# One modulation vector: sums on VectorE and a few selecting products in place of many narrow TensorE products

## The chip, the cores and the metric

The kernel runs on one core of one Trainium2 chip. The metric is the device time of one execution in microseconds (us). Three executions of the kernel before took 1913.95, 1915.27 and 1922.95 us; the median is 1915.27 us.

## The reference, cut to what matters

A two-layer backbone works on 256 latent tokens and 256 context tokens of width 2048. Each layer starts with a modulation:

```
mod   = silu(c)     @ mod_w[layer] + mod_b[layer]     # mod_w[layer]: 2048 x 6144
mod_c = silu(c_ctx) @ mod_w[layer] + mod_b[layer]
shift, scale, gate       = split(mod, 3)
shift_c, scale_c, gate_c = split(mod_c, 3)
h_lat = rms_norm(x)   * (1 + scale)   + shift
h_ctx = rms_norm(ctx) * (1 + scale_c) + shift_c
```

Layer 0 is a Hyena long convolution beside an S5 scan, layer 1 a differential attention. All is float32. The change touches one product only: the `scale` part of layer 1 (a 2048 x 2048 block of `mod_w[1]`), for the two streams latent (`c`) and context (`c_ctx`). It needs layer 1's weights and the two conditioning vectors and nothing else, so it can be worked out at any time before layer 1 begins.

## The kernel before, in words

Large products go by `project` and `rows`: a weight tile of 512 KB (128 partitions x 1024) is fetched on the SyncE queue into `raw` (three buffers), ScalarE rounds it to `whi` (L174), VectorE subtracts to `wlo` (L175), and TensorE makes three products (`mm3`, L108 to L110) of 512 columns for each of the tile's 8 pieces of 128 rows. `whi` and `wlo` have three buffers each, so VectorE can be at most some two to three tiles ahead of TensorE. A `unit` of layer 0's input projection is two such tiles, and in a `hp` unit two VectorE instructions of the short convolution after them (L760, L761).

Beside the units runs the generator `late()` (L708). It makes 48 steps: for layer 0's gate, layer 1's shift and layer 1's scale (`(layer, r)` = (0, 2), (1, 0), (1, 1)), for four blocks j of 512 columns, four steps i of 512 rows. A step first uses the two tiles `gw` of 512 KB that the step before had fetched, then asks for the next two; `gw` has two buffers, so a tile can be fetched only when the instructions that read its predecessor are done. Before the change a step is 16 calls of TensorE in `quarters` (L580): 128 rows of weights against the 32 columns of `cst` (columns 0 and 1 are the two streams), each for one quarter of 128 columns, into one PSUM bank `aux`. After four steps ScalarE copies the bank to the row `mrow` (L733). After four blocks `modulation` transposes it (L595) and adds the bias (L598, L624). Steps are started by `fill` inside `project`: half a step at each of a unit's two tiles while the Hyena stage runs, so about one step a unit.

The stage in which the last 16 steps (layer 1's scale) run is 718 to 965 us of the span: the end of the second of four Hyena quarters, ten units alone, then the last two Hyena quarters with the last units, then the start of the S5 gate (`glu`, whose tiles are multiplied by the pairs `gh`, `gl`).

The program is a fixed order of instructions for each engine, chosen when it is built. Each engine works through its own order and waits at the head of it; the same holds for the SyncE queue that issues the transfers. The gates of layer 1 are summed in the attention (L1142, L1144) by the same VectorE instruction that the change now uses for the scale.

Of the kernel before, what the change touches and what calls it, by code (L numbers as in the profile page):

```python
# [15 lines left out]
MULT, ADD, SUB = ALU.mult, ALU.add, ALU.subtract  # L16
# [128 lines left out]
def rsqrt(k, x, shape, tag):  # L145
    v = k.nc.vector
    y, t = k.t(shape, tag + "y", bufs=2), k.t(shape, tag + "t", bufs=2)
    k.nc.scalar.activation(t, x, AF.Sqrt)
    v.reciprocal(y, t)
    v.tensor_tensor(t, y, y, op=MULT)  # L150
    v.tensor_tensor(t, t, x, op=MULT)
    v.tensor_scalar(t, t, -0.5, 1.5, op0=MULT, op1=ADD)
    v.tensor_tensor(y, y, t, op=MULT)
    return y
# [341 lines left out]
def hybrid_kernel(ctx: ExitStack, tc: tile.TileContext, A, out):  # L496
    nc = tc.nc
    v, act, pe, dma = nc.vector, nc.scalar, nc.tensor, nc.sync
# [3 lines left out]
    k = K(tc, main, psum)  # L502

    def phase(name):
        class Phase:
            def __enter__(s):
                s.p = tc.tile_pool(name=name, bufs=1)
                k.pools.append(s.p.__enter__())

            def __exit__(s, *a):  # L510
                k.pools.pop()
                return s.p.__exit__(*a)
        return Phase()
# [15 lines left out]
    act.dma_start(pick, A["pick"])  # L529
    ones = k.m([128, 128], "ones")  # L530
    v.memset(ones, 1.0)
    even = phase("even")
    even.__enter__()
    P = k.e([128, 2, 8, 2, 4, 9], "s5P")
# [32 lines left out]
    def conditioning():  # L567

        t = k.e([128, 16, 32], "cst")
        v.memset(t, 0.0)  # L570
        for s in range(2):
            act.activation(t[:, :, s], cc[:, 16 * s:16 * s + 16], AF.Silu)
        return t

    cst = conditioning()

    def quarters(b, kk, w, first=0, last=15):

        for q in range(4):
            pe.matmul(b[32 * q:32 * q + 32, :128], cst[:, kk], w[:, q * 128:q * 128 + 128], start=kk == first, stop=kk == last)  # L580

    def modulation(layer, r, m):

        if r == 2:
            gate_rows(layer, m)
            return
        mods[layer, r] = (mod_scale if r else mod_columns)(layer, r, m)
# [88 lines left out]
    def project(W, col, h, lo_tok=0, n_tok=512, steps=0):  # L676

        b = k.bank("acc")
        nk = len(h)
        for kk, hi, lo in cols128(W, col, nk):  # L680
            s = slice(lo_tok, lo_tok + n_tok)
            mm3(nc, b[:, :n_tok], (hi, lo), (h[kk][0][:, s], h[kk][1][:, s]), kk == 0, kk == nk - 1)
            if kk % (nk // 2) == 0:
                fill(steps)
        return b
# [21 lines left out]

    def late():  # L708

        steps = [(layer, r, j, i) for layer, r in ((0, 2), (1, 0), (1, 1)) for j in range(4) for i in range(4)]  # L710

        def load(layer, r, j, i):
            ws = []
            for z in (2 * i, 2 * i + 1):
                w = k.e([128, 2, 512], "gw", bufs=GW)
                c0 = r * 2048 + j * 512
                dma.dma_start(w, A["mod_w"][layer][z * 256:z * 256 + 256, c0:c0 + 512].rearrange("(a p) m -> p a m", p=128))
                ws += [(2 * z + a, w[:, a]) for a in range(2)]
            return ws

        ws = load(*steps[0])
        for n, (layer, r, j, i) in enumerate(steps):
            yield
            if i == 0:
                b = k.bank("aux")
                if j == 0:
                    m = k.e([128, 512], "mrow", bufs=1)
            for kk, w in reversed(ws):
                quarters(b, kk, w, 3, 12)
            if n + 1 < len(steps):  # L730
                ws = load(*steps[n + 1])
            if i == 3:
                act.copy(m[:, j * 128:j * 128 + 128], b[:, :128])  # L733
                if j == 3:
                    modulation(layer, r, m)
        yield

    rest = late()

    due = [0]  # L740
# [34 lines left out]
    with phase("start"):  # L775
# [13 lines left out]
        for i, w in enumerate((w1, w2)):  # L789
            b = k.bank("wk")  # L790
            pe.matmul(b[:64, :256], w, prev, start=True, stop=True)
            z = k.t([64, 256], "hyz")
# [10 lines left out]
        for w in BLOCKS:  # L803
            c0 = sum(BLOCKS[:len(blocks)])
            blocks.append((c0, w))
            for r in (1, 0):
                kk = 0
# [178 lines left out]
    with phase("hyena"):  # L986
# [4 lines left out]
        for q in range(4):  # L991
# [20 lines left out]
            for i in range(2):  # L1012
# [3 lines left out]
                for part in range(2):  # L1016
                    bs = []
                    for e in range(2):
                        b = k.bank("wk")
# [38 lines left out]
            for c in range(2):  # L1058
                b = k.bank("tp", [128, 2, 2, 128])
# [17 lines left out]
    with phase("glu"):  # L1077
# [14 lines left out]
        for ct in range(8):  # L1092
            sg = k.t([128, 512], "sg", bufs=2)
            dma.dma_start(sg, spill["sg", ct])
            b = project(A["s5_glu_w"][0], ct * 128, gp)
# [27 lines left out]
    for i in range(2):  # L1123
        w = nw[:, i]
        v.tensor_tensor(tab[:, i, 0], rope[:, 0], w[:, None, :].to_broadcast([128, 2, 64]), op=MULT)
        for z in range(2):
            ws = w.rearrange("p (h z j) -> p h z j", h=2, z=2)[:, :, 1 - z][:, None].to_broadcast([128, 2, 2, 16])
# [116 lines left out]
    with phase("attention"):  # L1244
        hl = [x[1] for x in h]
        om = []
        for c in range(4):
# [6 lines left out]
            for hd in range(4):  # L1254
                b = project(W_in, 6144 + (c * 4 + hd) * 128, hl, 0, 256)
# [3 lines left out]
                for qt in range(2):  # L1259
                    z = k.t([128, 2], "z", bufs=4)  # L1260
                    mx = k.t([128, 2], "mx", bufs=4)
                    ps = []
                    for m in range(2):
                        b = k.bank("wk")
# [15 lines left out]
                for qt in range(2):  # L1280
                    qs = slice(qt * 128, qt * 128 + 128)
                    b = k.bank("wk")
# [3 lines left out]
                    r = k.t([128, 1], "or", bufs=2)  # L1286
                    act.activation(o2, b[:, :128], AF.Square, accum_out=r)
                    v.tensor_scalar(r, r, 1.0 / 128.0, EPS, op0=MULT, op1=ADD)
                    r = rsqrt(k, r, [128, 1], "ors")
# [33 lines left out]
def build(nc, inputs):  # L1323
    arrays, aps = {}, {}
    for name, a in list(inputs.items()) + list(constants().items()):
        a = np.ascontiguousarray(a)
        arrays[f"in_{name}_dram"] = a
        aps[name] = nc.dram_tensor(f"in_{name}_dram", a.shape, mybir.dt.from_np(a.dtype), kind="ExternalInput").ap()
    out = nc.dram_tensor("out_0_dram", (1, N, D), F32, kind="ExternalOutput").ap()
    with tile.TileContext(nc) as tc:  # L1330
        hybrid_kernel(tc, aps, out)
    return arrays
# [10 lines left out]
```

## Time and profile before

| what | value |
|---|---|
| median of three runs | 1915.27 us |
| the profiled execution | 1924.88 us |
| its span, first to last instruction | 1922.7 us |
| TensorE busy | 1841.3 us (96%) |
| VectorE busy | 1333.8 us (69%) |
| ScalarE busy | 790.2 us (41%) |
| mean granted TensorE clock | 0.988 of full speed |
| narrow products of L580 from `gw` | 2048 instructions, 88.9 us busy |

Matmuls overlap in their records, so what one costs is read from the distance between starts, not from its duration. A float32 product is two instructions in the trace: a step of 16 calls shows as 32. VectorE instructions overlap a little too.

### The profile page before, as it was taken

The page shows a single profiled execution, that of the slowest core. Times are in us where ns is not written, and L with a number is a line of the kernel's source. Part 1 is how long each engine was busy: PE and PEld are TensorE (multiplying, and loading weights), DVE is VectorE, ACT ScalarE, POOL GpSimd, SP SyncE. Part 2 cuts the span into 40 slices and gives each one's busy share as a digit, 9 for nine tenths or more (in the row PEclk, how much of TensorE's full clock was granted, in tenths as well). Part 3 has the DMA queues.
Part 4 walks back from the last instruction along what each step waited for, and adds up shares of the span by engine and source line. Part 5 has one row for each costly group of instructions (what it writes and reads, how often), then busy time and mean ns, then how long its engine had stood idle before and what let it go on. Part 6 is the DMA issues. An engine that isn't in the chain of part 4 may idle for free.

```text
span 1922.7 us, 30952 instructions
## 1 busy us (share of the span) xinstructions
PE 1841.3 (96%) x12101; PEld 1454.8 (76%) x12101; DVE 1333.8 (69%) x2563; ACT 790.2 (41%) x1245; POOL 7.0 (0%) x23
## 2 busy tenths in 40 slices
PE   4799899999999999999999999999999999999998
PEld 3577677777676677777788887779778878887977
DVE  4887768998985586258664347686866867768675
ACT  3342223222223332233352237537735833853762
POOL 0000000000000000000000000000000000000000
PEclk8899899999999999999999999999999999999999
DMA  9878655676875776564657345354336426435356
GB/s 302 263 248 265 215 147 164 181 236 200 246 226 149 247 236 194 187 210 157 215 188 234 113 139 178 100 167 139 103 107 186 121 88 190 131 96 170 127 178 227
DMA packets 325572, 349.57 MB, mean 182 GB/s; under 512 B 53417, under 2 KB 204459, under 8 KB 325427
## 3 DMA queue, kind: packets, MB, share of 16 engines
q1 hardware_dynamic: 314144, 339.84, 56.1%
q10 hardware_dynamic: 10850, 5.93, 1.2%
q8 instruction: 95, 1.56, 0.3%
q0 software_dynamic: 432, 1.84, 0.3%
q14 instruction: 51, 0.41, 0.1%
HBM read 316.06 MB, written 31.48 MB: 181 GB/s over the span
## 4 chain that ended last, share of the span: by engine, by line
PE 67%; DMA 4%; DVE 2%; ACT 1%; issue 1%; SPq 0%; ACTq 0%; DVEq 0%
PE ps_acc L108 14%; PE ps_acc L109 13%; PE ps_acc L110 13%; PE ps_aux L108 5%; PE ps_aux L109 5%; PE ps_aux L110 5%; DMA gw<-in_mod_w_dram 2%; PE ps_aux L580 2%; PE ps_wk L1266 2%; PE ps_wk L1284 2%; PE ps_wk L108 1%; PE ps_tp L1277 1%; PE ps_wk L109 1%; DVE wlo L175 1%; PE ps_wk L110 1%
## 5 line engine op out<-in xcount | busy, mean ns | idle before, releaser
L174 ACT CAST whi<-raw 128x1024 fp32r<-128x1024 f32 x304 | 318.8, 1049 | 640.6 <-PE ps_acc L109 341.1
L175 DVE TENSOR_TENSOR wlo<-raw,whi 128x1024 fp32r<-128x1024 f32 x304 | 371.4, 1223 | 303.0 <-ACT whi L174 298.7
L108 PE MATMUL ps_acc<-hhi,whi 128*128 128x512 f32 x768 | 313.9, 410 | 0.1
L109 PE MATMUL ps_acc<-hlo,whi 128*128 128x512 f32 x768 | 308.7, 402 | 0.2
L110 PE MATMUL ps_acc<-hhi,wlo 128*128 128x512 f32 x768 | 307.7, 401 | 0.0
L108 PEld LDWEIGHTS ps_acc<-hhi,whi 128*128 128x128 f32 x768 | 145.3, 190 | 42.7 <-issue 10.5
L110 PEld LDWEIGHTS ps_acc<-hhi,wlo 128*128 128x128 f32 x768 | 145.2, 189 | 34.6 <-issue 2.0
L109 PEld LDWEIGHTS ps_acc<-hlo,whi 128*128 128x128 f32 x768 | 145.3, 189 | 34.1 <-issue 3.2
L108 PE MATMUL ps_acc<-whi,hhi 128*128 128x512 f32 x416 | 165.9, 399 | 1.2 <-DVE qt L1167 0.9
L109 PE MATMUL ps_acc<-wlo,hhi 128*128 128x512 f32 x416 | 163.9, 394 | 0.0
L580 PE MATMUL ps_aux<-gw,cst 128*32 128x128 f32 x2048 | 88.9, 287 | 34.5 <-DMA gw<-in_mod_w_dram 30.3
L580 PEld LDWEIGHTS ps_aux<-gw,cst 128*32 128x32 f32 x2048 | 56.7, 113 | 69.2 <-DMA gw<-in_mod_w_dram 38.3
L108 PE MATMUL ps_aux<-whi,h 128*128 128x512 f32 x256 | 100.0, 393 | 4.8 <-DVE qt L1167 4.8
L109 PE MATMUL ps_aux<-wlo,h 128*128 128x512 f32 x256 | 101.1, 395 | 0.0
L110 PE MATMUL ps_acc<-whi,hhi 128*128 128x512 f32 x256 | 100.4, 392 | 0.0
L110 PE MATMUL ps_aux<-whi,h 128*128 128x512 f32 x256 | 100.4, 392 | 0.0
L108 PEld LDWEIGHTS ps_acc<-whi,hhi 128*128 128x128 f32 x416 | 78.2, 188 | 21.1 <-DVE qt L1167 2.9
L109 PEld LDWEIGHTS ps_acc<-wlo,hhi 128*128 128x128 f32 x416 | 78.3, 188 | 15.0
L110 PE MATMUL ps_acc<-whi,hlo 128*128 128x512 f32 x224 | 88.2, 394 | 0.0
L109 PE MATMUL ps_acc<-h,whi 128*128 128x256 f32 x256 | 72.7, 284 | 0.0
L108 PE MATMUL ps_acc<-h,whi 128*128 128x256 f32 x256 | 72.7, 284 | 0.0
L110 PE MATMUL ps_acc<-h,wlo 128*128 128x256 f32 x256 | 72.7, 284 | 0.0
(414 smaller groups left out, 3495.9 us busy)
## 6 DMA issues: line engine op xcount, KB each, us to landing
gw<-in_mod_w_dram SPq DMA_DIRECT2D x128, 512.0 KB
raw<-in_od_in_w_dram SPq DMA_DIRECT2D x128, 512.0 KB
raw<-in_ev_in_w_dram SPq DMA_DIRECT2D x96, 512.0 KB
raw<-in_ev_out_w_dram SPq DMA_DIRECT2D x40, 512.0 KB
hhi<-in_mod_w_dram SPq DMA_DIRECT2D x64, 256.0 KB
qt<-in_mod_w_dram SPq DMA_DIRECT2D x64, 256.0 KB
raw<-in_od_out_w_dram SPq DMA_DIRECT2D x32, 512.0 KB
spill_hp<-out SPq DMA_DIRECT2D x24, 256.0 KB
```

Of the source, the lines that this page charges most:

```text
L108: nc.tensor.matmul(out, lh, rh, start=start, stop=False)
L109: nc.tensor.matmul(out, lh, rl, start=False, stop=False)
L110: nc.tensor.matmul(out, ll, rh, start=False, stop=stop)
L174: k.nc.scalar.copy(hi, src)
L175: k.nc.vector.tensor_tensor(lo, src, hi.bitcast(F32), op=SUB)
L580: pe.matmul(b[32 * q:32 * q + 32, :128], cst[:, kk], w[:, q * 128:q * 128 + 128], start=kk == first, stop=kk == last)
L1266: pe.matmul(b, qT[m][part][:, hd, qt * 128:qt * 128 + 128], kT[m][:, hd], start=part == 0, stop=part == 1)
L1277: pe.transpose(tb[:, t], ps[0][:, t * 128:t * 128 + 128], ident)
L1284: pe.matmul(b[:, :128], wT[qt][:, t], vt[:, t, hd * 128:hd * 128 + 128], start=t == 0, stop=t == 3)
```

## The change

For `(layer, r)` = (1, 1) a step no longer calls `quarters`. VectorE keeps, for each of the 128 rows of a tile and each of the two streams, a running sum over the 16 pieces of 128 weight rows: `acc[row, stream, column]`, a tile of 128 x 2 x 512 that takes the place of `P` (tag `s5P`, one buffer). That is 8 instructions a step (4 pieces, 2 streams) on 512 columns: 2 of `tensor_scalar` at the start of each block j, else `scalar_tensor_tensor`. At the end of a block 8 products with `sel` (128 x 32, all zero but a column of ones at the stream's place) add up the 128 rows by quarters into the bank, which is now taken only there. The rest (copy, transposes, bias) is as before.

```diff
+    sel = k.m([128, 2, 32], "sel")
+    v.memset(sel, 0.0)
+    for s in range(2):
+        v.memset(sel[:, s, s:s + 1], 1.0)
...
             if i == 0:
-                b = k.bank("aux")
+                if (layer, r) != (1, 1):
+                    b = k.bank("aux")
+                else:
+                    acc = k.e([128, 2, 512], "s5P")
                 if j == 0:
                     m = k.e([128, 512], "mrow", bufs=1)
-            for kk, w in reversed(ws):
-                quarters(b, kk, w, 3, 12)
+            for z, (kk, w) in enumerate(reversed(ws)):
+                if (layer, r) != (1, 1):
+                    quarters(b, kk, w, 3, 12)
+                    continue
+                for s in range(2):
+                    if i == z == 0:
+                        v.tensor_scalar(acc[:, s], w, cst[:, kk, s:s + 1], None, op0=MULT)
+                    else:
+                        v.scalar_tensor_tensor(acc[:, s], w, cst[:, kk, s:s + 1], acc[:, s], op0=MULT, op1=ADD)
             if n + 1 < len(steps):
                 ws = load(*steps[n + 1])
+            if i == 3 and (layer, r) == (1, 1):
+                b = k.bank("aux")
+                for s in range(2):
+                    for q in range(4):
+                        pe.matmul(b[32 * q:32 * q + 32, :128], sel[:, s], acc[:, s, q * 128:q * 128 + 128], start=s == 0, stop=s == 1)
             if i == 3:
                 act.copy(m[:, j * 128:j * 128 + 128], b[:, :128])
```

How the order moves is shown at two places. (Line numbers of the changed kernel are 20 higher behind the change: L780 is L760, L1091 is L1071, L599 is L595; L744 and L742 are the new sums, L751 the selecting product.)

The first place is the fourth step of block 0, among the units that run alone (765 to 838 us in the trace before). VectorE there, before: two tiles and a convolution, over and over.

```order
L175 TENSOR_TENSOR wlo_7957<-raw_7954,whi_7956 128x1024
L760 SCALAR_TENSOR_TENSOR out_7861<-ps_acc_7780,pk_558_2737,out_7861 128x2x255
L761 SCALAR_TENSOR_TENSOR out_7861<-ps_acc_7780,pk_558_2737,out_7861 128x2x255
L175 TENSOR_TENSOR wlo_8008<-raw_8005,whi_8007 128x1024
L175 TENSOR_TENSOR wlo_8044<-raw_8041,whi_8043 128x1024
```

VectorE there, now (`gw_7710` and `gw_7708` are the third step's two tiles, `gw_7788` and `gw_7786` the fourth's; `s5P_7620` is the running sum of block 0):

```order
L175 TENSOR_TENSOR wlo_7938<-raw_7935,whi_7937 128x1024
L780 SCALAR_TENSOR_TENSOR out_7841<-ps_acc_7768,pk_559_2741,out_7841 128x2x255
L744 SCALAR_TENSOR_TENSOR s5P_7620<-gw_7708,cst_111,s5P_7620 128x512
L781 SCALAR_TENSOR_TENSOR out_7841<-ps_acc_7768,pk_559_2741,out_7841 128x2x255
L744 SCALAR_TENSOR_TENSOR s5P_7620<-gw_7708,cst_111,s5P_7620 128x512 x3
L175 TENSOR_TENSOR wlo_7981<-raw_7978,whi_7980 128x1024
L744 SCALAR_TENSOR_TENSOR s5P_7620<-gw_7788,cst_111,s5P_7620 128x512 x4
L175 TENSOR_TENSOR wlo_8017<-raw_8014,whi_8016 128x1024
L780 SCALAR_TENSOR_TENSOR out_7929<-ps_acc_7846,pk_559_2741,out_7929 128x2x255
L744 SCALAR_TENSOR_TENSOR s5P_7620<-gw_7786,cst_111,s5P_7620 128x512
L781 SCALAR_TENSOR_TENSOR out_7929<-ps_acc_7846,pk_559_2741,out_7929 128x2x255
L744 SCALAR_TENSOR_TENSOR s5P_7620<-gw_7786,cst_111,s5P_7620 128x512 x3
```

Every `wlo` but the first of these now stands behind four sums, and the sums behind a transfer of `gw`. TensorE at the same place, before, with a step's 16 calls between two products of a tile:

```order
L110 MATMUL ps_acc_7953<-hhi_794,wlo_7957 128x512
L580 MATMUL ps_aux_7963<-gw_7894,cst_107 32x128 x8
L580 MATMUL ps_aux_7963<-gw_7892,cst_107 32x128 x8
L108 MATMUL ps_acc_7953<-hhi_806,whi_7956 128x512
L109 MATMUL ps_acc_7953<-hlo_807,whi_7956 128x512
```

TensorE there, now:

```order
L110 MATMUL ps_acc_7934<-hhi_1836,wlo_7981 128x512
L751 MATMUL ps_aux_7868<-s5P_7620,sel_85 32x128 x4
L108 MATMUL ps_acc_7934<-hhi_1848,whi_7980 128x512
L109 MATMUL ps_acc_7934<-hlo_1849,whi_7980 128x512
L751 MATMUL ps_aux_7868<-s5P_7620,sel_85 32x128 x4
L110 MATMUL ps_acc_7934<-hhi_1848,wlo_7981 128x512
```

The steps' calls are gone, and block 0's selecting products stand behind the first products of the tile `wlo_7981`, while the last sums they read stand on VectorE behind the tile after it, `wlo_8017`.

The second place is the end of the last Hyena quarter and the beginning of the S5 gate (about 937 to 960 us in the trace before). VectorE before (`part`, `hyt`: the last Hyena instructions; `gl`: the low halves of the gate's inputs):

```order
L1071 TENSOR_TENSOR hyt_8874<-part_8680,hyt_8874 128x512
L175 TENSOR_TENSOR wlo_9431<-raw_9428,whi_9430 128x1024
L175 TENSOR_TENSOR gl_9223<-g_9220,gh_9222 128x512
L175 TENSOR_TENSOR wlo_9472<-raw_9469,whi_9471 128x1024
L175 TENSOR_TENSOR gl_9229<-g_9226,gh_9228 128x512
L175 TENSOR_TENSOR gl_9235<-g_9232,gh_9234 128x512
```

VectorE there, now:

```order
L1091 TENSOR_TENSOR hyt_8816<-part_8622,hyt_8816 128x512
L744 SCALAR_TENSOR_TENSOR s5P_8469<-gw_8840,cst_111,s5P_8469 128x512 x4
L744 SCALAR_TENSOR_TENSOR s5P_8469<-gw_8838,cst_111,s5P_8469 128x512 x4
L175 TENSOR_TENSOR gl_9142<-g_9139,gh_9141 128x512
L175 TENSOR_TENSOR gl_9148<-g_9145,gh_9147 128x512
L175 TENSOR_TENSOR gl_9154<-g_9151,gh_9153 128x512
L742 TENSOR_SCALAR s5P_8992<-gw_8916,cst_111 128x512 x2
L744 SCALAR_TENSOR_TENSOR s5P_8992<-gw_8916,cst_111,s5P_8992 128x512 x2
L744 SCALAR_TENSOR_TENSOR s5P_8992<-gw_8914,cst_111,s5P_8992 128x512 x4
L175 TENSOR_TENSOR gl_9160<-g_9157,gh_9159 128x512
L175 TENSOR_TENSOR gl_9166<-g_9163,gh_9165 128x512
```

The last step of block 2 and the first of block 3 have come to stand between the Hyena stage and the gate's inputs. TensorE there, before, at the gate's first tile:

```order
L595 MATMUL ps_tp_9369<-ident_79,mrow_7617 128x128 x3
L108 MATMUL ps_acc_9427<-gh_9222,whi_9430 128x512
L109 MATMUL ps_acc_9427<-gl_9223,whi_9430 128x512
L110 MATMUL ps_acc_9427<-gh_9222,wlo_9431 128x512
L108 MATMUL ps_acc_9427<-gh_9228,whi_9430 128x512
```

TensorE there, now:

```order
L1082 MATMUL ps_tp_8806<-ident_79,hyt_8797 128x128
L599 MATMUL ps_tp_9281<-ident_79,mrow_7621 128x128 x2
L751 MATMUL ps_aux_8918<-s5P_8469,sel_85 32x128 x8
L108 MATMUL ps_acc_9339<-gh_9141,whi_9342 128x512
L599 MATMUL ps_tp_9281<-ident_79,mrow_7621 128x128
L109 MATMUL ps_acc_9339<-gl_9142,whi_9342 128x512
```

Block 2's selecting products stand right behind the last Hyena transposes and ahead of every product of the gate.

## Rows read from the trace of the kernel before

**Rows 1.** The page: busy time by engine, and busy tenths in 40 slices.
```profile
PE 1841.3 (96%) x12101; PEld 1454.8 (76%) x12101; DVE 1333.8 (69%) x2563; ACT 790.2 (41%) x1245; POOL 7.0 (0%) x23
...
PE   4799899999999999999999999999999999999998
...
DVE  4887768998985586258664347686866867768675
```
**Rows 2.** Stretches: PE, PEld, DVE, ACT, POOL busy (instructions), clock, DMA share, GB/s.
```profile
765.00:838.00 73.00, 73.00 (x453) 57.80 (x450) 19.58 (x20) 15.54 (x19) 0.00 (x0) 1.00 0.62 195
838.00:965.00 127.00, 125.43 (x764) 96.49 (x764) 93.47 (x109) 46.65 (x66) 0.00 (x0) 1.00 0.61 197
...
718.00:965.00 247.00, 245.43 (x1496) 190.37 (x1496) 144.63 (x166) 77.05 (x102) 0.00 (x0) 1.00 0.61 196
```
**Rows 3.** Waits in 718 to 965 us: us in total, times, longest.
```profile
DVE wlo L175 <- ACT whi L174: 69.5, 24, 5.6
...
PE ps_aux L580 <- DMA gw<-in_mod_w_dram: 1.6, 1, 1.6
```
**Rows 4.** TensorE in order of time around one step: start, us, instruction.
```profile
763.62 0.40 PE L110 MATMUL ps_acc<-hhi,wlo 128*128 128x512 f32 x1
763.94 1.08 PE L580 MATMUL ps_aux<-gw,cst 128*32 128x128 f32 x32
764.95 0.50 PE L108 MATMUL ps_acc<-hhi,whi 128*128 128x512 f32 x1
765.29 0.39 PE L109 MATMUL ps_acc<-hlo,whi 128*128 128x512 f32 x1
765.52 0.40 PE L110 MATMUL ps_acc<-hhi,wlo 128*128 128x512 f32 x1
```
**Rows 5.** In order of time: one tile's split among the lone units.
```profile
769.92 1.05 ACT L174 CAST whi<-raw 128x1024 fp32r<-128x1024 f32 x1 [5.04 <-PE ps_acc L109]
771.00 1.23 DVE L175 TENSOR_TENSOR wlo<-raw,whi 128x1024 fp32r<-128x1024 f32 x1 [4.09 <-ACT whi L174]
```
**Rows 6.** TensorE's group of narrow products in 718 to 965 us.
```profile
L580 PE MATMUL ps_aux<-gw,cst 128*32 128x128 f32 x512 | 19.5, 277 | 1.6 <-DMA gw<-in_mod_w_dram 1.6
```
**Rows 7.** Sums of layer 1's gate: ns min/median/max; in time; their waits.
```profile
L1142 DVE TENSOR_SCALAR gsum<-qt,sc x4: 485/486/488, 1278.7 to 1757.0; 128x512 f32<-128x512 f32 x4
...
1292.84 3.11 DVE L1144 SCALAR_TENSOR_TENSOR gsum<-qt,sc,gsum 128x512 f32<-128x512 f32 x4
...
DVE gsum L1144 <- DMA qt<-in_mod_w_dram: 16.8, 12, 2.0
```
**Rows 8.** VectorE in order of time: independent instructions one behind the other.
```profile
750.63 0.68 DVE L1065 TENSOR_TENSOR part<-ps_tp,part 128x512 f32<-128x512 f32 x1
751.22 0.74 DVE L761 SCALAR_TENSOR_TENSOR out<-ps_acc,pk,out 128x510 f32<-128x510 f32 x1
751.88 0.68 DVE L1065 TENSOR_TENSOR part<-ps_tp,part 128x512 f32<-128x512 f32 x1
...
847.70 2.35 DVE L1034 TENSOR_TENSOR hyz<-hyU,hyK 128x1024 f32<-128x1024 f32 x2
849.97 1.22 DVE L1035 TENSOR_TENSOR hyy<-hyy,hyz 128x1024 f32<-128x1024 f32 x1
```
**Rows 9.** Transfers of `gw` on the chain of waits: start, us to landing.
```profile
513.58 5.36 DMA gw<-in_mod_w_dram
...
662.04 7.50 DMA gw<-in_mod_w_dram
```
**Rows 10.** In order of time: SyncE's issue for block 0; VectorE's instruction ahead of it.
```profile
718.60 0.38 SPq L717 DMA_DIRECT2D gw<-in_mod_w_dram  x1
...
723.90 0.69 DVE L1052 TENSOR_TENSOR hyt<-ps_wk,hyt 128x512 f32<-128x512 f32 x1 [0.91 <-PE ps_wk L110]
```
**Rows 11.** The clock behind a stop of TensorE: its first instruction, then the stretch.
```profile
669.58 0.43 PE L580 MATMUL ps_aux<-gw,cst 128*32 128x128 f32 x2 [2.57 <-DMA gw<-in_mod_w_dram]
...
669.50:673.20 3.70, 3.62 (x10) 2.09 (x11) 0.65 (x2) 0.59 (x1) 0.00 (x0) 0.54 0.04 15
```

## The prediction, on record before the result was known

> **What bounds the kernel now.** I read the page's busy times and slices first, then the stretch of the change by windows, then its waits, then single instructions. TensorE is busy 96% of the span and 9 tenths or more in nearly every slice; VectorE has 69% overall, but it is uneven [rows 1]. The last 16 steps of `late()` run in 718 to 965 us. There TensorE is busy 245.4 of 247 us at full clock, so whatever leaves its order there shortens the time, and whatever makes it wait lengthens it one for one [rows 2]. VectorE has 144.6 us of work in these 247, but 19.6 of 73 in the lone units (765 to 838) and 93.5 of 127 in the two Hyena quarters behind them [rows 2]. Of its idle time 69.5 us is waiting at `wlo` for ScalarE's `whi`: that is being ahead, since `whi` itself waits until TensorE frees a buffer [rows 3]. So VectorE is not late today, and its lead is what the change draws on.
>
> How large is the lead? Products start 0.233 us apart, a tile of 24 takes 5.6 us [rows 4]. `whi` begins at 769.92, when the tile three back is freed, and `wlo` ends at 772.2; TensorE gets there two tiles later, at 781.1. The lead is at most 8.9 us [rows 4, 5].
>
> **What goes.** A step's 32 instructions push the products apart: from L110 at 763.62 to L109 at 765.29 are 1.67 us where two distances of 0.233 would do, so a step costs 1.21 us [rows 4], and 16 steps 19.4 us; the group's 19.5 us busy for 512 instructions agrees [rows 6]. One wait of 1.6 us for `gw` goes with them [rows 3]. The selecting products that come are 8 calls a block, half a step: 0.7 us with one seam more, 2.8 us for four blocks. TensorE's order gets 19.4 + 1.6 - 2.8 = 18.2 us shorter. The three memsets at the start are too small to count.
>
> **What comes.** VectorE gets 120 `scalar_tensor_tensor` and 8 `tensor_scalar`. The same two instructions sum layer 1's gate: four sums in a chain take 3.11 us, 0.79 apart, and the first of a chain 0.49 [rows 7]. Here neighbours belong to two streams and don't wait for each other; an instruction of that kind beside independent ones starts 0.66 after its start [rows 8]. So a sum is bounded by 0.66 and 0.79, and I take 0.66, the nearer case; the 8 cheap ones at 0.40. Together 82 us (99 at the other end), in a stretch where VectorE idles 102 us, 69.5 of it as lead. By totals it just fits. By place it does not, because of what the sums wait for and what waits behind them.
>
> A sum waits for its `gw` tile. Two buffers hold exactly one step, so a tile is asked for only when the sums of its predecessor's buffer end. Before, a step read both tiles in one burst of 1 us and the transfer had the rest of a 12 us unit. Now the readers are spread over VectorE's order. Landing took 5.36 to 7.50 us [rows 9]; these transfers had company, so I take 5.4.
>
> The page "DMA: Bandwidth & Descriptors" of the Trainium skill (section "Anatomy of one DMA") fits a transfer with 2.0 us plus bytes over 436 GB/s, by my estimate 3.2 us for 512 KB. The rows above disagree, at 5.4 and more. By 3.2 us each of some seven waits below would be 2.2 us shorter and the result about 1937 us; the fit is for another queue, and I don't use it.
>
> Now the places, in order of time.
>
> (a) The first sums stand behind the second `hyt` of a Hyena quarter, which ends at 724.6, and ahead of a low half that TensorE's Fourier products need; their tile is asked for at 718.6 and lands by the longer row at 726.1 [rows 9, 10]: 1.5 us late (0 by the shorter row, 3 with the sums themselves).
>
> (b) Lone units. After `wlo_7981` VectorE must wait for `gw_7788`, asked for when the sums just ahead of `wlo_7981` end: 5.4 - 1.1 = 4.3 us. Then four sums 2.6, `wlo_8017` 1.1 (tiles start the next instruction after 1.13 [rows 8]), two of the convolution 1.3, four sums 2.6: 12 us until block 0 is summed. TensorE's order has the selecting products behind the first products of the tile `wlo_7981`, so TensorE stands still while two tiles lie ready or nearly so: 12 less its lead. The full lead of 8.9 leaves 3 us. But the same round (5.4 + 2.6 + 1.1 + 1.3 + 2.6 = 13.0 us a unit, against TensorE's 11.2) eats 1.8 us of lead a unit; with 3 left it is 9 us. I take 6. Block 1 ends the same way, behind the first product of a tile with two `wlo` and nine sums after it: 6 (2 to 10).
>
> (c) The last two Hyena quarters. VectorE has 93.5 us of work in 127 [rows 2]; 24 sums, three steps, stand in its order before the gate's inputs. Counted by its rows at 1.13, 0.61 and 0.66 [rows 8], the stretch from the tile at which the quarters begin to the last Hyena tile takes 87 us, of which 15 are sums, plus one bare wait for `gw` (the step after a tile's last sum: 3 us) and the chain's own waits for ScalarE and TensorE, of which I keep 5. TensorE's rows there are 82 us at 0.233. VectorE is the bound: 95 - 82, less what lead is left: 10 us (5 to 18).
>
> (d) The end of block 2. TensorE does the last Hyena transposes, then the selecting products. VectorE does `part` and `hyt` (four, 2.4), waits for `gw_8840` (asked for late: 3.5), sums eight (5.3): TensorE stands 11. Then three `gl` (1.8), a wait for `gw_8916` (4.5), eight sums (4.8) come ahead of `gl_9160`, and TensorE has only products with the first three `gl`, 27 of them, 6.3 us: another 5. With the late `g` transfers, 18 us (12 to 25). In the order before, this stretch stopped TensorE for 1.6 us only.
>
> (e) Block 3's other three steps stand in the gate: tiles that take TensorE 5.6 us each meet four to eight sums and a wait of 0.5 to 3.5 us each, and the last selecting products wait behind two whole steps, 16 sums and four low halves (17 us with waits) where TensorE has one tile: 10 us (5 to 15).
>
> (f) After a stop of 2.57 us the granted clock was 0.54 for 3.7 us, so about 1.7 us is lost a second time [rows 11]. Four stops are that long; where TensorE is waiting anyway it costs nothing: 5 us (0 to 10).
>
> Sum: 1.5 + 6 + 6 + 10 + 18 + 10 + 5 = 56.5, less 18.2: 38 us slower. The profiled execution took 1924.88 us; with the change it would take 1963. The median of the runs shown is 9.6 lower, 1915.27, so I predict 1953 us. The low ends add to 27, the high ends to 90: 9 to 72 us slower, 1924 to 1987.
>
> **Rivals.** *Full cover:* VectorE's lead hides every sum, and TensorE keeps its gain: 1915.3 - 18.2 = 1897 us. For it: 102 us idle against 82 us of new work, and no more bytes. Against it: the last selecting products, which need sums that stand behind the tile TensorE is working at. It would need transfers that land within about 3 us and a lead that is always full.
>
> *Break-even:* the waits are real but small: landing in 4 us, stops of 3 (b), 0 (c), 12 (d), 5 (e): 20 against 18.2, 1917 us. For it: the gate's sums in the attention waited for their transfers only 16.8 us in all, at most 2.0 at a time [rows 7], though with four buffers.
>
> *Collapse:* VectorE's queue is the bound from block 0 on: landing 7.5 us makes the round 15.1 us against 11.2, seven units lose 27 instead of 12, (c) to (e) take their high ends, 58, and each restart its 1.7 us with more stops: 12. With (a) that is 100 - 18 = 82, 1997 us. The page "TensorE: Matmul & The Clock Gate" of the Trainium skill (section "What's actually happening") has the clock fall to 1.2 GHz when TensorE has been idle; rows 11 agree with 0.54, and by that rule scattered stops cost twice. Against it: a starved TensorE that runs slowly waits less.
>
> **Chances.** Forecast (15 to 65 slower) 0.66, collapse 0.13, break-even 0.12, full cover 0.09. A change below 0.5%, 9.6 us, can't be told from none here. Break-even counts as the same, full cover as faster, the rest as slower: 0.09, 0.12, 0.79. The range 1916 to 1986 leaves out full cover and most of the collapse.
>
> **What would show it.** VectorE at 9 tenths in the slices from 720 to 1000 us, with its waits at L742 and L744 named as `gw` transfers, 3 to 6 us each and some 50 us in all; TensorE with stops at L751 (four, the third the longest) and at products with `gl`; L580 with 1536 instructions from `gw`; a granted clock below 1 there. I am wrong if L751 shows hardly a wait, if the sums start as close as 0.6 with the tile always landed, or if the time between the last lone unit and the gate grows by less than 10 us.

## The result and the profile after

| kernel | median us | against the kernel before (95% interval) |
|---|---|---|
| before | 1916.71 (4 runs) | |
| changed | 1939.91 (4 runs, 1936.12 to 1940.01) | 1.0099 (1.0078 to 1.0120) |

By the ratio the change makes the kernel 1.0% slower, 19 us (15 to 23). The two medians are 23 us apart, the two profiled executions 15. The forecast was 38 us slower, 1953.

The page of the changed kernel, busy time by engine and the busy tenths of the 40 slices (48.4 us each), answers to [rows 1]:

```profile
PE 1835.0 (95%) x11653; PEld 1449.1 (75%) x11653; DVE 1411.7 (73%) x2694; ACT 790.3 (41%) x1245; POOL 7.0 (0%) x23
...
PE   4799899999999999999689999999999999999999
...
DVE  4887778999984788689775337776866767777675
```

TensorE is busy 6.3 us less in a span that is 15.1 us longer (1937.8 us). Its only new hole is in the two slices from 920 to 1017 us (6 and 8 tenths). Of the slices from 720 us on VectorE is at 9 tenths in one only, the one ahead of the hole (872 to 920 us); I had said all of them up to 1000. The stretches of [rows 2], cut finer, in the changed kernel (columns as there):

```profile
718.00:765.00 47.00, 46.86 (x207) 37.08 (x206) 39.53 (x52) 14.04 (x17) 0.00 (x0) 1.00 0.59 184
765.00:838.00 73.00, 67.93 (x311) 52.45 (x310) 52.09 (x71) 18.09 (x25) 0.00 (x0) 0.95 0.65 196
838.00:900.00 62.00, 61.84 (x274) 48.72 (x273) 57.12 (x71) 21.29 (x28) 0.00 (x0) 1.00 0.53 164
900.00:965.00 65.00, 50.08 (x215) 37.56 (x214) 54.70 (x73) 21.43 (x30) 0.00 (x0) 0.87 0.53 169
965.00:1030.00 65.00, 57.07 (x235) 44.62 (x234) 47.03 (x68) 24.35 (x34) 0.00 (x0) 0.89 0.49 157
```

Up to 900 us TensorE (first busy column) misses 5.4 us of 182; behind 900 us it misses 22.9 of 130, at a clock of 0.87 and 0.89. The waits answer to [rows 3]: VectorE's in 718 to 1030 us, then TensorE's in 718 to 1060 us.

```profile
DVE s5P L744 <- DMA gw<-in_mod_w_dram: 22.5, 11, 4.8
DVE wlo L175 <- ACT whi L174: 13.3, 12, 2.4
DVE s5P L742 <- DMA gw<-in_mod_w_dram: 4.4, 3, 3.1
```
```profile
PE ps_aux L751 <- DVE s5P L744: 16.2, 5, 10.7
PE ps_acc L108 <- ACT si L1117: 7.1, 2, 4.2
```

The sums wait for `gw` 27 us, where I had said some 50. VectorE's lead, 69.5 us of waiting at `wlo` in 718 to 965 us before, has shrunk to 8.8 there (13.3 up to 1030 us). The four largest stops of TensorE, in order of time:

```profile
785.58 0.65 PE L751 MATMUL ps_aux<-s5P,sel 128*32 128x128 f32 x8 [3.51 <-DVE s5P L744]
...
950.86 1.32 PE L751 MATMUL ps_aux<-s5P,sel 128*32 128x128 f32 x16 [10.67 <-DVE s5P L744]
...
962.53 0.80 PE L109 MATMUL ps_acc<-gl,whi 128*128 128x512 f32 x1 [2.85 <-DVE gl L175]
...
1008.00 0.80 PE L108 MATMUL ps_acc<-gh,whi 128*128 128x512 f32 x1 [4.25 <-ACT si L1117]
```

The third block's selecting products (950.86) are the place of step (d), with the length it gave, 11 us. But the chain of waits through that stop shows more than sums (start, us, what). It leads through the handover, the passage from the Hyena stage's results to the gate's inputs:

```profile
938.42 0.79 PE ps_tp L1082 x6
939.22 5.49 DMA hyt<-spill_hg
944.83 0.70 DVE hyt L1091
945.55 2.03 DMA mscr<-hyt
947.78 2.72 DMA g<-gscr
950.72 0.76 DVE s5P L744
951.49 5.41 DMA gw<-in_mod_w_dram
```

The last Hyena result leaves by `mscr`, only then is `g`, the gate's first input, fetched, and that lands at 950.5, just when the sums end. (The sum at 950.72 reads no `g`; the chain only puts one behind the other.) Ahead of its eight sums VectorE had waited 3.3 us for the transfer of `hyt` and 0.6 us for `gw`, where (d) had 3.5 us for `gw`. Whether the sums or `g` held TensorE can't be read from the stop; that was the first question for the runs.

The calls of L580 are gone as told: 512 fewer [rows 6]. The line, L584 now, has over the whole span:

```profile
L584 PE MATMUL ps_aux<-gw,cst 128*32 128x128 f32 x1536 | 70.1, 293 | 29.1 <-DMA gw<-in_mod_w_dram 24.9
```

### The profile page after: what moved, and what is told of

Its sections match the earlier page's. It is cut to its first block, busy times and chain, and to the rows that moved or that the text cites. A ratio compares the mean times of both kernels' runs of the same rounds, so it can differ in the third digit from the quotient of the medians.

```text
span 1937.8 us, 30202 instructions
## 1 busy us (share of the span) xinstructions
PE 1835.0 (95%) x11653; PEld 1449.1 (75%) x11653; DVE 1411.7 (73%) x2694; ACT 790.3 (41%) x1245; POOL 7.0 (0%) x23
## 4 chain that ended last, share of the span: by engine, by line
PE 58%; DVE 4%; DMA 4%; ACT 1%; issue 1%; SPq 0%; DVEq 0%; ACTq 0%; POOLq 0%
PE ps_acc L108 12%; PE ps_acc L109 12%; PE ps_acc L110 12%; PE ps_aux L108 5%; PE ps_aux L109 5%; PE ps_aux L110 5%; DMA gw<-in_mod_w_dram 3%; PE ps_wk L1286 2%; PE ps_wk L1304 2%; DVE s5P L744 2%; DVE wlo L175 1%; PE ps_tp L1297 1%; PE ps_wk L108 1%; PE ps_tp L1204 1%; PE ps_wk L109 1%
## 5 line engine op out<-in xcount | busy, mean ns | idle before, releaser
L108 PE MATMUL ps_acc<-hhi,whi 128*128 128x512 f32 x768 | 312.1, 407 | 0.1
L108 PEld LDWEIGHTS ps_acc<-hhi,whi 128*128 128x128 f32 x768 | 145.1, 189 | 40.7 <-issue 7.9
L108 PE MATMUL ps_acc<-whi,hhi 128*128 128x512 f32 x416 | 165.6, 399 | 1.3 <-DVE qt L1187 0.9
L108 PE MATMUL ps_aux<-whi,h 128*128 128x512 f32 x256 | 100.0, 393 | 4.8 <-DVE qt L1187 4.8
L744 DVE SCALAR_TENSOR_TENSOR s5P<-gw,cst,s5P 128x512 f32<-128x512 f32 x120 | 83.1, 744 | 22.5 <-DMA gw<-in_mod_w_dram 22.5
L584 PE MATMUL ps_aux<-gw,cst 128*32 128x128 f32 x1536 | 70.1, 293 | 29.1 <-DMA gw<-in_mod_w_dram 24.9
L108 PEld LDWEIGHTS ps_acc<-whi,hhi 128*128 128x128 f32 x416 | 78.2, 188 | 22.2 <-DVE qt L1187 2.9
L584 PEld LDWEIGHTS ps_aux<-gw,cst 128*32 128x32 f32 x1536 | 44.0, 115 | 55.4 <-DMA gw<-in_mod_w_dram 32.5
L108 PE MATMUL ps_acc<-h,whi 128*128 128x256 f32 x256 | 72.7, 284 | 0.0
```

The source lines that it names most:

```text
L108: nc.tensor.matmul(out, lh, rh, start=start, stop=False)
L744: v.scalar_tensor_tensor(acc[:, s], w, cst[:, kk, s:s + 1], acc[:, s], op0=MULT, op1=ADD)
```

## The experiments

All are compared with the kernel before on the same chip; us are the ratio's difference from 1 times 1921, the median of before there (minus is faster). The theories in capitals are those that the expectations set against each other. "Cover" is the number of dense products (three to an `mm3`, 0.233 us each) which the order leaves TensorE between the last Hyena transposes and the first product of the gate: 75 in the kernel before, none in the changed one.

| run | cover | ratio (interval) | us |
|---|---|---|---|
| changed | 0 | 1.0099 (1.0078 to 1.0120) | +19 |
| no_sums | 46 | 0.9896 (0.9876 to 0.9916) | -20.0 |
| one_load | 8 | 0.9965 (0.9945 to 0.9984) | -6.7 |
| free_products | 0 | 1.0071 (1.0049 to 1.0093) | +13.6 |
| blocks01 | 87 | 0.9980 (0.9965 to 0.9995) | -3.8 |
| blocks23 | 8 | 1.0050 (1.0031 to 1.0069) | +9.6 |
| hyena_earlier | 93 | 1.0036 (1.0019 to 1.0053) | +6.9 |
| before_earlier | 219 | 1.0030 (1.0011 to 1.0049) | +5.8 |
| before_uncovered | 0 | 1.0219 (1.0194 to 1.0244) | +42 |
| early_sums | 0 | 1.0046 (1.0029 to 1.0064) | +8.8 |
| pool_queue | 10 | 1.0136 (1.0110 to 1.0161) | +26 |
| blocks01_earlier | 94 | 0.9994 (0.9977 to 1.0011) | -1.2 |
| blocks012_earlier | 93 | 0.9976 (0.9962 to 0.9991) | -4.6 |

**What TensorE gains.** no_sums:

```diff
-            for s in range(2): ... tensor_scalar / scalar_tensor_tensor on acc
-                ws = load(*steps[n + 1])      # for (1, 1)
-    pe.matmul(b[...], sel[:, s], acc[:, s, ...], ...)
+    pe.matmul(b[...], sel[:, s], ones, ...)
```

> Leaves out layer 1's scale: for (1, 1) neither transfers of gw nor sums; the selecting products read a tile of ones. This is TensorE's side of the change alone. By the prediction's first term the 16 steps' calls go (19.4 us) with one wait (1.6), and the selecting products come (2.8): 18 us faster than before, about 1898. If the stretch was in truth held by something else than TensorE's order (a transfer of weights, say), the gain is under 10 us.

Measured: 20.0 us faster. The first term stands; everything else the change does costs 39 us.

**Which blocks.** blocks01 and blocks23:

```diff
-                if (layer, r) != (1, 1):
+                if ((layer, r) != (1, 1) or j >= 2):      # blocks23: j < 2
```

> Sums on VectorE for blocks 0 and 1 only; blocks 2 and 3 by the narrow products as before. Theory END: the loss is where blocks 2 and 3 are summed, between the last Hyena quarter and the gate; the first two blocks are covered but for two stops of 3.5 and 1.6 us: 9.7 less 1.4 less some 5, that is 2 to 5 us faster than before (1912 to 1915). Theory VOLUME (each sum costs the same, since VectorE's queue is what delays TensorE) and theory ROUND (waits for gw with two buffers, in the lone units most of all): half of the loss or more, 10 to 15 us slower (1927 to 1932).

> Sums for blocks 2 and 3 only. Theory END: the whole loss and none of the gain of the first half, 24 to 30 us slower than before (1941 to 1947), with the stop of about 10 us at the selecting product of block 2. VOLUME: half, 10 to 13 us slower. ROUND: under 10 us slower, since the lone units have no sums.

Measured: -3.8 us, as END had it and neither VOLUME nor ROUND, and +9.6, where END had 24 to 30 and the other two about 10. No theory has both. The halves add to 5.8 and the whole is 19, so the loss is not a sum over blocks. In blocks23 TensorE never waits for `si`, and the gate takes 58.7 us from its first to its last product (changed kernel 68.5, before 46.0).

**Sum or input.** free_products has the second half of no_sums' edit alone: sums and transfers stay.

> All transfers and sums stay, but the selecting products read a tile of ones, so TensorE never waits for a sum (the sums' result is left out). If END works through the products that stand ahead of the gate's work (16 us of stops at L751 and the half clock behind them): about 16 to 20 us under the changed kernel, 1920 to 1924. If END works through the gate's inputs and sg that stand behind the sums and behind the gw transfers: at most 6 us under it, 1934 or more.

Measured: 5.4 us under the changed kernel, 1935 us: the second way. (The two intervals overlap, so that the 5.4 may be less; 16 to 20 would have shown.) With nothing to wait for at the selecting products, TensorE stands at the next instruction:

```profile
941.63 0.66 PE L599 MATMUL ps_tp<-ident,mrow 128*128 128x128 f32 x4 [0.82 <-DVE part L1085]
955.49 1.22 PE L108 MATMUL ps_acc<-gh,whi 128*128 128x512 f32 x2 [13.21 <-DMA g<-gscr]
```

So the stop that the trace puts down to the sums is `g`'s as well. The kernel before has the same chain (`mscr` issued at 941.8, `gh` at 949.0 and its first product at 956.1) with 75 dense products, 17.5 us, to do meanwhile. From the last Hyena transposes to the first `gh` it takes 12.0 us there (937.0 to 949.0) and 11.7 in the changed kernel (939.0 to 950.7), so the sums have not made the chain longer; what is gone is the work beside it. From here on theory COVER said that the changed order has spent these products earlier.

**Giving cover back, and taking it away.** hyena_earlier, and the same edit on the kernel before as control:

```diff
+            with tc.high_priority(offset=200) if q >= 2 else nullcontext():
                 ...   # the Hyena quarter's own instructions, not the units behind it
```

before_uncovered does the opposite to the kernel before:

```diff
+                with tc.high_priority(offset=400):   # last quarter's units and the gate's one
                     unit(*u, STEPS_H)
```

> The changed kernel, all sums kept, but the last two Hyena quarters are given an earlier place (a priority 200 lower) when the order is made. By its order 93 dense products (21.7 us at 0.233) stand between the last Hyena transposes and the first product of the gate, where the changed kernel has none and the kernel before 75; g is issued ahead of the fourth step of block 2 on SyncE. Theory COVER (the loss is that nothing is left for TensorE while part, hyt, mscr, g and gh follow one another, 12 to 15 us with the half clock behind it): 10 to 18 us under the changed kernel, 1922 to 1930. Theory SUMS (VectorE's added work has to be paid at the end of the Hyena stage wherever it is put): the time goes back into the Hyena quarters as waits for VectorE, 1936 to 1944.

> The kernel before, with the last two Hyena quarters given the same earlier place as in the run hyena_earlier (priority 200 lower): the control for that run. By its order 219 dense products are left behind the last Hyena transposes, where 75 were enough. COVER, by which cover beyond the need is worth nothing: within 4 us of before, so that what hyena_earlier won was lost cover regained. If the earlier place is worth something by itself: 8 us or more faster.

> The kernel before with its narrow products and no sum on VectorE; only the last five units of the input projection are given an earlier place (a priority 400 lower), so that no dense product (75 in the kernel before) stands between the last Hyena transposes and the gate. COVER: TensorE stands some 10 to 13 us there and works at half clock for a while: 10 to 18 us slower than before. SUMS, or a theory by which the SyncE queue is held by gw transfers that wait for sums: no change, within 4 us.

Measured: hyena_earlier is 12 us under the changed kernel (1928 us), and the order by itself wins nothing (+5.8, a little outside what I allowed). before_uncovered is 42 us slower without a single sum, far over the 10 to 18: its order uncovers not only the handover (8.0 us at `gh`) but the whole last quarter (19.6 us in four waits at `yh`). It shows that an uncovered handover stops TensorE without a single sum, but not what that costs in the changed kernel. In hyena_earlier the stop at the handover is gone, and still its gate takes 69.3 us from its first to its last product (68.5 in the changed kernel, 46.0 before), at the same low clock (columns as in [rows 2]):

```profile
939.20:1009.30 70.10, 57.09 (x242) 43.05 (x241) 53.71 (x79) 25.55 (x38) 0.00 (x0) 0.88 0.58 189
```

So the handover is one loss and the gate another, which cover does not give back. The section behind the experiments comes back to it.

**Sums elsewhere.** early_sums:

```diff
-        ... for layer, r in ((0, 2), (1, 0), (1, 1)) ...
+        ... for layer, r in ((0, 2), (1, 1), (1, 0)) ...
```

> The changed kernel with layer 1's scale summed 16 steps earlier, ahead of layer 1's shift (whose narrow products come last): no sum stands near the gate. By its order no dense product stands between the last Hyena transposes and the gate (32 narrow calls do, some 3 us, if their gw is there). SUMS, QUEUE and the prediction's step (d): the loss at the end goes, 8 to 16 us under the kernel before. COVER: the stop of 8 to 12 us stays, so no better than 6 us under before and up to 6 over it.

Measured: +8.8 (5.6 to 12.3), over both expectations, though the interval reaches COVER's 6, and against every theory that lays the whole loss to sums near the gate; 10 of the changed kernel's 19 us do go. The handover was open without them: last transposes at 954.4, first product of the gate at 966.45, in between the shift's narrow products with a wait of 6.25 us for their own `gw`.

**The transfers.** one_load fetches 2 of the 32 tiles; pool_queue issues them elsewhere:

```diff
-            if n + 1 < len(steps):
+            if n + 1 < len(steps) and steps[n][:2] != (1, 1):
                 ws = load(*steps[n + 1])
```
```diff
-                dma.dma_start(w, ...)
+                (nc.gpsimd if (layer, r) == (1, 1) else dma).dma_start(w, ...)
```

> The changed kernel without the transfers: of layer 1's scale only the first step's two tiles are fetched, and all 16 steps sum those again (so the scale is of the wrong weights). VectorE's 128 sums and the selecting products stay; no sum waits for gw, and no gw issue stands on SyncE's queue ahead of g and sg. By its order 8 dense products stand between the last Hyena transposes and the gate. Theory GW (the two buffers, the landing and SyncE's queue are the loss, as the prediction has it in (b), (d), (e)): 5 to 15 us faster than before. COVER: the chain from the last transposes to gh stays open (8 to 12 us); what gw cost in front (some 4 us) and behind (7 us of stops at si) goes: level with before to 8 us slower.

> The changed kernel with layer 1's scale tiles gw issued on the GpSimd queue, so that an issue that waits for a sum holds up nothing on SyncE (g, sg, mixed, weights). By its order 10 dense products and 12 more instructions stand behind the last Hyena transposes. Theory QUEUE (the gw issues ahead of g and sg on SyncE are the loss): 10 to 20 us under the changed kernel. COVER: 3 to 7 us under it, since g still follows mscr.

Measured: one_load -6.7, within GW's range and not COVER's; but COVER's stop is there, with no `gw` on its way and by chance of the same 10.67 us (TensorE in order of time, then the chain of waits, in one_load):

```profile
940.86 1.22 PE L108 MATMUL ps_acc<-gh,whi 128*128 128x512 f32 x2 [10.67 <-ACT gh L174]
```
```profile
932.04 0.61 DVE hyt L1091
932.67 4.56 DMA mscr<-hyt
937.37 2.71 DMA g<-gscr
940.19 0.63 ACT gh L174
```

Each theory holds a part. And the sums by themselves, 105 of the 128 by then, cost TensorE nothing (one_load, columns as in [rows 2]):

```profile
718.00:928.00 210.00, 209.57 (x957) 166.32 (x958) 195.44 (x251) 65.58 (x85) 0.00 (x0) 1.00 0.41 126
```

VectorE is busy 195 of 210 us and TensorE 209.6. Theory VOLUME falls. pool_queue is 7 us slower than the changed kernel, where QUEUE had 10 to 20 faster: taking the issues off SyncE's queue gives nothing back. What the other queue costs by itself was not measured. A round in the lone units, from a step's first sum to the next step's, is 13.7 us (769.70 to 783.36) on this queue, and the longest on SyncE's is 13.8 (764.56 to 778.36); pool_queue's selecting products waited longer, 26.9 us. Landing takes 4.6 us there, and 4.1 to 5.8 on SyncE's by the changed kernel's chain of waits (pool_queue's page; the last number is the median us from issue to landing):

```profile
gw<-in_mod_w_dram POOLq DMA_DIRECT2D x32, 512.0 KB, 4.6
```

The fit of the Trainium skill that the prediction set aside (page "DMA: Bandwidth & Descriptors", section "Anatomy of one DMA") is for this queue and gives an estimate of 3.2 us for 512 KB; the measured 4.6, with other transfers under way, decides.

**A version that beats both.** blocks01_earlier and blocks012_earlier have blocks01's edit (the second with `j >= 3`) and hyena_earlier's (offset 100 and 200).

> Sums for blocks 0 and 1 only, and the last two Hyena quarters a priority 100 earlier: 94 dense products behind the last transposes. A version meant to beat both. COVER: the gain of the first two blocks (4 to 8 us faster than before) and no loss at the end, 1912 to 1917 where before is 1921.

> Sums for blocks 0 to 2, the narrow products for block 3, and the last two Hyena quarters a priority 200 earlier: 93 dense products behind the last transposes. COVER: block 2's sums meet a covered end, so it gains on blocks 0 and 1 by up to 4.2 us more (block 2's calls 4.9, less selecting products 0.7) or loses some 5 at the selecting products: 12 us faster to level with before. VOLUME (each sum costs 0.15 us wherever it stands, 23 us over 128): 3/4 of the loss, over 10 us slower.

Measured: -1.2, which is no gain, and -4.6. The latter is 24 us under the changed kernel and 0.24% under the one before, and the noise doesn't tell it from blocks01 alone (0.20%). Its stops in 718 to 1060 us are short:

```profile
PE ps_aux L584 <- DMA gw<-in_mod_w_dram: 3.5, 3, 1.3
PE ps_aux L751 <- DVE s5P L744: 2.9, 2, 1.5
```

## Why the prediction was right in sign and too large in size

Four traces, cut at the same marks: the first transposes of the first and of the third Hyena quarter (both behind the same dense products in all four), the gate's first and last L108 with `gh`. Us from mark to mark:

| | first to third quarter | to the gate | the gate | sum |
|---|---|---|---|---|
| before | 202.0 | 118.5 | 46.0 | 366.5 |
| no_sums | 192.0 | 110.4 | 46.8 | 349.3 |
| one_load | 192.7 | 120.1 | 46.2 | 359.0 |
| changed | 196.5 | 124.6 | 68.5 | 389.7 |

The columns "to the gate" and "the gate" of the changed kernel and of one_load come from these groups (start of the first and of the last) and the transposes at 827.48 and 820.79:

```profile
L108 PE MATMUL ps_acc<-gh,whi x64: 387/389/796, 952.1 to 1020.6; 128*128 128x512 f32 x64
```
```profile
L108 PE MATMUL ps_acc<-gh,whi x64: 388/390/797, 940.9 to 987.1; 128*128 128x512 f32 x64
```

The changed kernel loses 40.4 us on no_sums: 4.5 in the first column, 14.2 in the second, of which 9.7 remain when nothing is transferred, 21.7 in the gate, of which none does. (2.8 of the 21.7 are not lost: the changed kernel's gate holds 202 dense products and that of the other three 190, as its order has drawn 12 in from behind.) Over the runs the gate's length goes with the number of sums that start in it, and not with the cover in front of it (hyena_earlier 93, changed none):

| run | sums in the gate | the gate, us |
|---|---|---|
| early_sums | 0 | 44.8 |
| no_sums | 0 | 46.8 |
| one_load | 7 | 46.2 |
| free_products | 27 | 58.6 |
| blocks23 | 24 | 58.7 |
| pool_queue | 32 | 65.4 |
| changed | 32 | 68.5 |
| hyena_earlier | 37 | 69.3 |

In one_load the sums wait for no tile, so most of them are done before the gate begins. It therefore doesn't tell whether the sums themselves or their transfers make the gate long. By the prediction's terms:

- *Removed, -18.2:* measured -20.0. Right.
- *The sums' duration:* taken at 0.66, eight in a row took 5.39 us at 993.99, 0.66 apart. Right, as [rows 8] had it and not [rows 7].
- *(a) and (b), 1.5 + 12:* measured 4.5 with the clock in the first column, and 1.6 in the second: 6.1. (a) hardly stopped TensorE at all (0.14 us idle in 718 to 765). (b)'s stops are where they were put, 3.51 us at 785.58 and 1.57 at 830.87, not 6 and 6. The transfers were as taken (5.84 and 4.78 us on the chain of waits among the lone units, against [rows 9]) but the round of 13.0 was reached twice only, at 13.8 and 13.0; the five rounds from 764.56 to 826.08 take 12.3 on average. What failed is the step that spent VectorE's lead at 1.8 us a unit until it was gone. Three waits for `gw` in a row, 2.16, 3.47 and 4.83 us, came to no more than the one stop of 3.51, and later VectorE waits for `whi` again, which is being ahead (VectorE in order of time in the changed kernel):

```profile
764.56 2.74 DVE L744 SCALAR_TENSOR_TENSOR s5P<-gw,cst,s5P 128x512 f32<-128x512 f32 x4 [3.47 <-DMA gw<-in_mod_w_dram]
...
778.36 2.74 DVE L744 SCALAR_TENSOR_TENSOR s5P<-gw,cst,s5P 128x512 f32<-128x512 f32 x4 [4.83 <-DMA gw<-in_mod_w_dram]
```

- *(c), 10 (5 to 18):* this step failed. TensorE lost next to nothing in the last two Hyena quarters, 0.16 us of 62 between 838 and 900. The bound of 95 us against 82 has too few products for TensorE: 82 us are 352 of them, about what the order before has from the third quarter's first transposes to the last ones (357), and the new order has 432 there, 101 us. The 75 more are the very ones that had been the cover. The time came back behind them, as a handover without cover. One of the prediction's signs of being wrong came about with it: from the last lone unit to the gate the time grew by 6.1 us (second column), less than 10.
- *(d), 18 (12 to 25):* 10.67 + 2.85 = 13.5 us of stops. The place and the first stop's length (11) are right; the cause is half right, since `hyt`, `mscr` and `g` take as long: 10.67 us in one_load with no wait for `gw`, 13.21 in free_products with no sum waited for. That the size fits so well is in part luck.
- *(e), 10 (5 to 15):* 2.83 + 4.25 us at `si` and under 1 at L751 and `wlo`. The size holds, the place does not: TensorE is not stopped by a tile's `wlo` or at the last selecting products, as (e) had it, but at the bank that `si` should empty. `si` waits for `sg` (L1118), that for its transfer, issued only at 1002.55, once `hlo` had freed its buffer, and `hlo` stood behind eight sums (rows of the changed kernel, VectorE's and SyncE's in order of time):

```profile
993.99 5.39 DVE L744 SCALAR_TENSOR_TENSOR s5P<-gw,cst,s5P 128x512 f32<-128x512 f32 x8 [1.79 <-DMA gw<-in_mod_w_dram]
...
1001.84 1.28 DVE L175 TENSOR_TENSOR hlo<-sg,hhi 128x512 fp32r<-128x512 f32 x2
1006.48 0.69 DVE L1118 TENSOR_TENSOR sg<-sg,si 128x512 f32<-128x512 f32 x1 [3.36 <-DMA sg<-spill_sg]
```
```profile
1002.55 8.39 SPq L1114 DMA_DIRECT2D sg<-spill_sg  x4
```

- *(f), 5 (0 to 10):* too small. In the gate alone TensorE is busy 12.9 us longer, at a clock of 0.86; 2.8 of that are the 12 dense products more. The handover's stop needn't be there for it: hyena_earlier has none, and its gate is as long at 0.88. The stretch in the changed kernel, then in the one before:

```profile
952.10:1021.10 69.00, 57.73 (x226) 43.88 (x223) 50.05 (x74) 25.41 (x37) 0.00 (x0) 0.86 0.56 184
```
```profile
956.10:1002.50 46.40, 44.83 (x227) 36.71 (x226) 30.03 (x41) 24.07 (x35) 0.00 (x0) 1.00 0.64 212
```

So 13.5 that came to 6.1 and 10 that came to none are 17 of the 19 us between forecast and result; (d), (e) and (f), 33 in the sum, came to 31.5 by the second and third column without (b)'s 1.6 and the 2.8 of work moved in. That this sum is so near is partly luck, as (e) had another place and (f) was too small. Of the rivals, *full cover* had the gain right and the cost wrong, and one_load shows what it wanted: with the tiles landed, VectorE hides the sums up to the handover. *Collapse* needed a queue that is the bound from block 0 on, and VectorE was not.

Open stay which of the two, the sums or their transfers, holds up the gate; why the halves add to 5.8 and not 19; and what put the 75 products early: the order was made knowing the sums, and moving Hyena ahead takes 12 us back, but which of its rules did it was not tried.

## What to carry to other kernels

Work moved to an idle engine can cost little by its volume (one_load); here it cost by what it had to wait for and by what waited behind it in order: about half of what the changed kernel lost on no_sums it lost in the gate, among the 32 sums that stand there. In a fixed order look for the handover between two stages and count the filling work that the new order leaves there: 75 products hid a chain of three transfers, and none were left after a change that touches no instruction of that chain. A trace names the last of several waits, so take that one away on its own before you call it the cause.

## What was not expected of the hardware

The clock stayed low for longer than [rows 11] suggested: after the stop of 10.67 us the granted clock was 0.50, the lower level of 1.2 GHz, while the selecting products ran, and 0.64 still at 965 to 970 us, 14 us after work had begun again, with short stops of 0.2 and 2.85 us between (the changed kernel, columns as in [rows 2]).

```profile
945.00:952.00 7.00, 1.14 (x16) 0.41 (x16) 6.44 (x11) 1.14 (x2) 0.00 (x0) 0.50 0.56 174
952.00:958.00 6.00, 5.75 (x20) 3.50 (x16) 2.34 (x6) 1.31 (x3) 0.00 (x0) 0.76 0.97 346
958.00:965.00 7.00, 3.92 (x12) 2.85 (x12) 7.00 (x12) 3.69 (x7) 0.00 (x0) 0.77 0.75 246
965.00:970.00 5.00, 5.00 (x16) 3.93 (x15) 2.27 (x4) 1.72 (x3) 0.00 (x0) 0.64 0.67 237
```

In one_load a stop as long was followed by 0.59 in the first 5 us and then by full speed, without further stops:

```profile
941.00:946.00 5.00, 5.00 (x14) 3.93 (x15) 4.68 (x8) 3.49 (x6) 0.00 (x0) 0.59 1.01 336
946.00:951.00 5.00, 5.00 (x24) 4.14 (x23) 4.96 (x8) 4.22 (x6) 0.00 (x0) 1.00 0.33 128
```

That the short stops kept it down is what these two traces suggest, and hyena_earlier with them, whose gate has a clock of 0.88 with stops of 3.5 us at most; no run took the short stops away alone. The Trainium skill (page "TensorE: Matmul & The Clock Gate", section "What's actually happening") has 1.2 GHz for an idle TensorE; the 0.50 agrees.
